# Gate and upper halves of an FFN as seven products of block sums, in two phases with the activations in DRAM

## The chip, the cores and the metric

The kernel runs on one core of a Trainium2 chip. The metric is the device time of one execution in microseconds (us). It is taken over several runs, and the median stands for the kernel. One further execution is profiled.

## The reference

One layer of a hybrid decoder: a normalised input goes through one projection into a chunk-gating group, a stick-breaking attention and a forgetting attention, their outputs through one output projection, and then through a dense SwiGLU FFN. The change touches the FFN alone, for 1024 prompt rows and 64 sample rows (1088 tokens), a model width of 1024 and an inner width of 2816:

```python
def swiglu(x, w_in, w_out):
    h = x @ w_in
    return (jax.nn.silu(h[..., :D_FF]) * h[..., D_FF:]) @ w_out
...
        yp = yp + swiglu(rms_norm(yp, g_ffn[l]), w_ffn_in[l], w_ffn_out[l])
...
        ys = ys + swiglu(rms_norm(ys, g_ffn[l]), w_ffn_in[l], w_ffn_out[l])
...
    y_prompt = rms_norm(yp, g_final)
```

## The kernel before

Every large product is made of three matmuls, since each fp32 operand is split into a rounded part ("hi", an ACT cast) and the remainder ("lo", a DVE or POOL subtraction): hi by hi, hi by lo and lo by hi. PE accumulates them in a PSUM bank. The order of the instructions on every engine is set by a scheduler that simulates the program; the code gives the order of buffers and the priorities.

Ahead of the FFN the output projection ends (`product`, tile prod, L1147 to L1150): the residual sits in y, nine row tiles of 128 tokens in SBUF. `step` normalises a finished row tile (L190, L196) and `spread` transposes it on PE (L204), casts it on ACT into xh2 (L206) and subtracts on DVE into xl2 (L207). The last weights of the output projection are loaded as wor (L1134), cast on ACT (L1137) and split on DVE (L1138).

The FFN loop runs over the 22 slices of 128 inner columns, in 11 pairs (FCH = 2). For each slice, the gate's and the upper weights (128x1024, tile fraw_) are loaded by SP's queue (L1308), cast by ACT (fh, L1311), and the remainder taken by DVE (fl, L1312). For each of three token chunks (384, 384 and 320 columns) and both halves there are 8 times 3 matmuls into a bank of tag fgu (L1326 to L1328). ACT takes the silu of the gate's bank (L1331), DVE multiplies the upper bank by it (L1332), ACT casts the product into g_h (L1333) and POOL takes the remainder g_l (L1335). After two slices the output weights, split in the same way, follow: for nine row tiles and two halves of 512 columns the matmuls fout (L1359, L1360 and L1362), 104 for each pair, and DVE adds each bank to y (L1363). Tag fgu has three of the eight banks, fout and the transposes the other five. Behind the last pair the squares, the scale and the output rows follow (L1279 to L1296), DVE and POOL sharing the rows.

Of the kernel before, what the change touches and what calls it, by code (L numbers as in the profile page):

```python
# [10 lines left out]
F32 = mybir.dt.float32  # L11
# [7 lines left out]
D = 1024  # L19
# [11 lines left out]
FCH = 2  # L31
_TC = {"schedule_with_timeline_sim": True}
# [64 lines left out]
def tile_decode_step(ctx, tc, x_prompt, x_sample, cache_sb_k, cache_sb_v, cache_fox_k, cache_fox_v,  # L97
# [55 lines left out]
    fsn = dr.tile([6, 64], F32, name="fsn")  # L153

# [924 lines left out]
    def merge(mp, y):  # L1079
# [63 lines left out]
        def product(gi, i, hf, xs, ws, o, meanwhile=None):  # L1143
# [9 lines left out]
            V.scalar_tensor_tensor(y[0:n, i, hs], pm[0:n], rr[0:n, gi, i:i + 1], y[0:n, i, hs], op0=OP.mult,  # L1153
# [21 lines left out]
        for j, gi in enumerate(ORDER):  # L1175
            for hf in range(2):
                nxt = ORDER[j + 1] if hf and j < 2 else None
                for ci in range(3):
# [40 lines left out]
    ypool = pool(ctx, "ypool", side="right")  # L1219
    y = ypool.tile([128, NTILE, D], F32, name="y")  # L1220
# [3 lines left out]
    G.memset(y[64:128, 8], 0.0)  # L1224
# [21 lines left out]

    def step(lag):
        if whole_:
            i = whole_.pop(0)
            if i == 8:  # L1250
                t = xin.tile([128, D], F32, name="xs2", tag="xs2", bufs=XSB)
                A.copy(t[0:64], y[64:128, 8])
                V.tensor_tensor(y[0:64, 8], y[0:64, 8], t[0:64], op=OP.add)
                G.memset(y[64:128, 8], 0.0)
            xn.append((i, norm(y[:, i], rows(i), gfb, xin)))
        if len(xn) > lag:
            i, x2 = xn.pop(0)
            spread(x2, rows(i), i, xh2, xl2)
# [4 lines left out]
    whole(8)  # L1263
    pmp.close()
    wfst = ExitStack()
    wf = pool(wfst, "wf", side="right")

    sums = {}

    def square(i, hf):  # L1270

        n, hs = rows(i), slice(hf * 512, hf * 512 + 512)
        jk = wf.tile([128, D], F32, name="fraw_", bufs=3)
        if i == 8:
# [23 lines left out]
    for f0 in range(0, NFF, FCH):  # L1298
# [4 lines left out]
        for ff in range(f0, f0 + nf):  # L1303
            ws_ = []
            for half in range(2):
                c0 = half * DFF + ff * 128
                raw = wf.tile([128, KT, 128], F32, name="fraw_", bufs=3)
                S.dma_start(raw, w_ffn_in[0, :, c0:c0 + 128].rearrange("(k p) c -> p k c", p=128))  # L1308
                h_ = wf.tile([128, KT, 128], F32R, name="fh", bufs=3)
                l_ = wf.tile([128, KT, 128], F32R, name="fl", bufs=3)  # L1310
                A.copy(h_, raw)  # L1311
                V.tensor_tensor(l_, raw, f(h_), op=OP.subtract)  # L1312
                ws_.append((h_, l_))
# [83 lines left out]
```

## Time and profile before

| | us |
|---|---|
| three runs | 1647.5, 1649.11, 1650.43 (median 1649.11) |
| profiled execution, its own time | 1652.82 |
| its span, first to last instruction | 1651.1 |
| PE busy in the span | 1559.6 |
| DVE, ACT, POOL busy | 862.3, 627.7, 474.7 |
| mean granted clock of TensorE, as a share | 0.976 |

Busy time is the sum of an engine's instructions. Matmuls overlap in the records: one is shown from its start to a modelled end, though the next starts earlier, so their pace is read from starts. The timeline gives start, length, engine, line, and what was written and read, with the buffer's number left out. A bracket at a row's end tells how long the engine was idle and what released it.

### The profile page before, as it was taken

What the parts mean: (1) busy time and instruction counts of PE and PEld (TensorE: products, weight loads), DVE (VectorE), ACT (ScalarE), POOL (GpSimd) and SP (SyncE); (2) the same over time, 40 slices, a digit from 0 to 9 for tenths busy, and PEclk for the clock granted to TensorE, in tenths of its full rate; (3) what the DMA queues carried; (4) which work ended last, traced back from release to release, by engine and by line L of the source; (5) the groups of instructions that cost most, each with busy time, mean ns of one, the idle gap of its engine ahead of it and who ended that gap; (6) DMA issues with size and microseconds to landing.
All of it is one profiled execution on the core that took longest, in us unless ns stands there. A gap on an engine that the chain in (4) does not pass through costs nothing.

```text
span 1651.1 us, 23878 instructions
## 1 busy us (share of the span) xinstructions
PE 1559.6 (94%) x8980; PEld 1439.6 (87%) x8980; DVE 862.3 (52%) x1565; ACT 627.7 (38%) x1291; POOL 474.7 (29%) x596
## 2 busy tenths in 40 slices
PE   6999999798799989888999999999999999999997
PEld 6999998697588878777889999898998989999895
DVE  5433369767688978787683332413333242333316
ACT  6424256555477878744362112120111212111114
POOL 1203275546355654464211001010100101010013
PEclk9999999999899989999999999999999999999999
DMA  5255565447867865854222111111110111111002
GB/s 174 56 168 180 187 187 147 114 134 236 222 204 227 234 182 165 290 175 127 88 83 84 39 38 52 44 45 41 52 52 26 52 51 42 36 52 51 26 1 108
DMA packets 137303, 184.54 MB, mean 112 GB/s; under 512 B 17844, under 2 KB 110372, under 8 KB 137188
## 3 DMA queue, kind: packets, MB, share of 16 engines
q1 hardware_dynamic: 127924, 132.48, 27.1%
q0 software_dynamic: 9264, 50.53, 9.6%
q8 instruction: 71, 1.16, 0.3%
q14 instruction: 44, 0.36, 0.1%
HBM read 147.50 MB, written 35.47 MB: 111 GB/s over the span
## 4 chain that ended last, share of the span: by engine, by line
PE 52%; DVE 2%; DMA 2%; issue 1%; POOL 0%; ACT 0%; SPq 0%; DVEq 0%; POOLq 0%; ACTq 0%
PE fgu L1326 11%; PE fgu L1328 11%; PE fgu L1327 11%; PE fout L1360 5%; PE fout L1359 5%; PE fout L1362 5%; PE prod L1147 1%; PE prod L1148 1%; DMA lr<-linv 1%; PE prod L1150 1%; DMA wor<-in_w_o_dram 0%; DVE fl L1294 0%; PE spread L204 0%; DVE vh L812 0%; DVE cr L1107 0%
## 5 line engine op out<-in xcount | busy, mean ns | idle before, releaser
L1328 PE MATMUL fgu<-xh,fl 128*128 128x384 f32 (+1 forms) x1056 | 345.9, 328 | 1.0 <-DVE fl L1312 1.0
L1326 PE MATMUL fgu<-xh,fh 128*128 128x384 f32 (+1 forms) x1056 | 345.4, 328 | 0.8 <-ACT xh L206 0.5
L1327 PE MATMUL fgu<-xl,fh 128*128 128x384 f32 (+1 forms) x1056 | 345.7, 327 | 0.0
L1335 POOL TENSOR_TENSOR g_l<-sl,g_h 128x384 fp32r<-128x384 f32 (+1 forms) x66 | 75.1, 1138 | 672.9 <-ACT g_h L1333 672.9
L1363 DVE TENSOR_TENSOR y<-fout,y 128x512 f32<-128x512 f32 x198 | 135.6, 690 | 127.9 <-PE fout L1362 115.9
L1326 PEld LDWEIGHTS fgu<-xh,fh 128*128 128x128 f32 x1056 | 198.1, 188 | 2.9 <-ACT xh L206 0.8
L1328 PEld LDWEIGHTS fgu<-xh,fl 128*128 128x128 f32 x1056 | 198.3, 188 | 2.2 <-DVE fl L1312 1.3
L1327 PEld LDWEIGHTS fgu<-xl,fh 128*128 128x128 f32 x1056 | 198.3, 188 | 0.7
L1332 DVE TENSOR_TENSOR sl<-fgu,sl 128x384 f32<-128x384 f32 (+1 forms) x66 | 35.3, 535 | 301.4 <-PE fgu L1328 301.4
L1360 PE MATMUL fout<-fol,g_h 128*128 128x512 f32 x396 | 156.6, 395 | 0.0
L1359 PE MATMUL fout<-foh,g_h 128*128 128x512 f32 x396 | 156.5, 395 | 0.0
L1362 PE MATMUL fout<-foh,g_l 128*128 128x512 f32 x352 | 139.1, 395 | 0.0
L812 POOL TENSOR_TENSOR vh<-vr,vh 128x384 fp32r<-128x384 f32 x96 | 102.4, 1083 | 80.0 <-ACT vh L811 59.7
L1333 ACT CAST g_h<-sl 128x384 fp32r<-128x384 f32 (+1 forms) x66 | 32.6, 493 | 184.6 <-DVE sl L1332 184.6
L743 PE MATMUL sqk<-kt,qz 128*128 128x512 f32 x288 | 99.3, 439 | 3.0 <-DVE ats L800 1.2
L286 PE MATMUL pqk<-xh,wh 128*128 128x384 f32 (+1 forms) x288 | 97.0, 337 | 1.2 <-DVE pvt L599 0.6
L287 PE MATMUL pqk<-xl,wh 128*128 128x384 f32 (+1 forms) x288 | 95.5, 333 | 0.0
L288 PE MATMUL pqk<-xh,wl 128*128 128x384 f32 (+1 forms) x288 | 94.8, 333 | 0.0
L1360 PEld LDWEIGHTS fout<-fol,g_h 128*128 128x128 f32 x396 | 74.3, 188 | 16.7
L1359 PEld LDWEIGHTS fout<-foh,g_h 128*128 128x128 f32 x396 | 74.3, 188 | 16.7
L582 PE MATMUL apv<-at,vv 128*128 128x256 f32 x432 | 76.2, 299 | 10.3 <-DVE hl L302 4.8
L572 DVE TENSOR_TENSOR at<-atr,at 128x512 fp32r<-128x512 f32 (+2 forms) x144 | 76.3, 543 | 16.1 <-ACT at L571 15.5
(436 smaller groups left out, 3302.3 us busy)
## 6 DMA issues: line engine op xcount, KB each, us to landing
qq<-qs SPq DMA_DIRECT2D x36, 256.0 KB
wraw<-in_w_in_dram SPq DMA_DIRECT2D x20, 384.0 KB
kk<-ks SPq DMA_DIRECT2D x24, 256.0 KB
vs<-vt SPq DMA_DIRECT2D x16, 384.0 KB
vv<-vs SPq DMA_DIRECT2D x12, 512.0 KB
wor<-in_w_o_dram SPq DMA_DIRECT2D x22, 256.0 KB
qs<-hl SPq DMA_DIRECT2D x12, 384.0 KB
ks<-hl SPq DMA_DIRECT2D x12, 384.0 KB
```

The costliest lines, as they stand in the source:

```text
L286: T.matmul(pm[:, 0:n], lhsT=wh, rhs=xh[:, k, o], start=k == 0, stop=False)
L287: T.matmul(pm[:, 0:n], lhsT=wh, rhs=xl[:, k, o], start=False, stop=False)
L288: T.matmul(pm[:, 0:n], lhsT=wl, rhs=xh[:, k, o], start=False, stop=k == KT - 1)
L743: T.matmul(pz, lhsT=queries(p, a, si), rhs=kts[t][p][:, b], start=si == 0 and p == 0 and n_ == 0, stop=si == 1 and p == 2 and n_ == 2)
L812: (V if t >= 16 and j in VL else G).tensor_tensor(vh[:, 1], vrs[t][:, j], f(vh[:, 0]), op=OP.subtract)
L1326: T.matmul(pm[:, 0:n], lhsT=h_[:, k], rhs=xh2[:, k, o], start=k == 0, stop=False)
L1327: T.matmul(pm[:, 0:n], lhsT=h_[:, k], rhs=xl2[:, k, o], start=False, stop=False)
L1328: T.matmul(pm[:, 0:n], lhsT=l_[:, k], rhs=xh2[:, k, o], start=False, stop=k == KT - 1)
L1359: T.matmul(pm, lhsT=gh[q][:, o], rhs=wh2[q][:, hs], start=q == 0, stop=False)
L1360: T.matmul(pm, lhsT=gh[q][:, o], rhs=wl2[q][:, hs], start=False, stop=i == 8 and end)
L1362: T.matmul(pm, lhsT=gl[q][:, o], rhs=wh2[q][:, hs], start=False, stop=end)
L1363: V.tensor_tensor(y[:, i, hs], pm, y[:, i, hs], op=OP.add)
```

## The change

The two halves of the FFN's input weights are cut into blocks: the 8 groups of 128 model rows into two blocks of four, gate and upper columns as the two column blocks, and the 1088 tokens into two halves of 544 columns (HT). A block product of two by two by two blocks needs eight products; here it is made of seven products of sums of blocks, with additions on both sides. The code names them q = 1 to 7.

Weight sums: `wsum` makes four sums of 128x512 on POOL for each slice j. `split` makes hi and lo of the seven weight operands (ACT cast L1321 and DVE subtraction L1322, 128x512 each). Token sums: `token_sums` makes, once, the operands of q = 5, 6, 7 and 4 in tiles th and tl, from the spread tokens, which now lie in four tiles each of xh and xl; 4 block rows by 2 column chunks, DVE and POOL taking parts (L1420 to L1434). Products: `product` (L1335 to L1337) makes 12 matmuls of 272 columns in an fgu bank, for seven q and two chunks c, so 14 products for each slice and 308 in all. `first` holds q = 1, 2, 3, `second` q = 6, 5, 7, 4; in the loop `first` of slice j + 1 stands ahead of `second` of slice j. The results are joined: L1353 (ga), L1364 (u2), L1367 (t), L1376 (u3), L1378 and L1385 on DVE, all reading a bank; two additions, one of them beside each silu of ACT, and two multiplications in each chunk on POOL. The bank of q = 5 is read twice, by L1367 and, once q = 7 is there, by L1378.

Two phases: the finished activations ga and gb of a slice are stored to DRAM (gs, two transfers per slice), and y's row tiles 0 to 7 are stored to ysc as soon as they are normalised, and their SBUF room is released for the weights. After the 22 slices all of phase one's room is released; y comes back (tiles z0 to z7, L1480), and the second phase loads for each slice the output weights (L1519) and its activations (L1521), splits them (L1524 to L1530), and runs the fout matmuls and additions as before, in pairs.

```diff
 FCH = 2
+HT = NTOK // 2
+RAWB, WSB, FOB = 2, 8, 4
...
+    gs = [dr.tile([128, NTOK], F32, name=f"gs{j}") for j in range(NFF)]
+    ysc = [dr.tile([128, D], F32, name=f"ysc{i}") for i in range(8)]
...
+            if i < 8:
+                S.dma_start(ysc[i], y[i])
...
+    def wsum(j):
+        ga_, up = raws[j]
+        g1, g2, u1, u2 = ga_[:, 0:4], ga_[:, 4:8], up[:, 0:4], up[:, 4:8]
...
+        G.tensor_tensor(s1, u1, u2, op=OP.add)
+        G.tensor_tensor(s2, s1, g1, op=OP.subtract)
+        G.tensor_tensor(s4, g2, s2, op=OP.subtract)
+        G.tensor_tensor(s3, g1, u1, op=OP.subtract)
+        sums[j] = {1: g1, 2: g2, 3: s4, 4: u2, 5: s1, 6: s2, 7: s3}
+
+    def split(j, q):
...
+        A.copy(x[:, 0], src)
+        V.tensor_tensor(x[:, 1], src, f(x[:, 0]), op=OP.subtract)
...
+    NP = ((0, HT // 2), (HT // 2, HT))
+    FIRST, SECOND = (1, 2, 3), (6, 5, 7, 4)
...
+    def product(j, q, c):
...
+        pm = bank([128, 512], "fgu")
+        for k in range(4):
+            T.matmul(pm[:, 0:b - a], lhsT=w[:, 0, k], rhs=hi[:, k, a:b], start=k == 0, stop=False)
+            T.matmul(pm[:, 0:b - a], lhsT=w[:, 0, k], rhs=lo[:, k, a:b], start=False, stop=False)
+            T.matmul(pm[:, 0:b - a], lhsT=w[:, 1, k], rhs=hi[:, k, a:b], start=False, stop=k == 3)
...
+    def second(j, q, c):
+        pm = product(j, q, c)
...
+        elif q == 5:
+            t = temp("t", 3)
+            V.tensor_tensor(t, pm, held[j, c, "u2"], op=OP.add)
...
+            G.tensor_tensor(o, t, held.pop((j, c, 3)), op=OP.add)
+            A.activation(o, o, AF.Silu)
+            held[j, c, 5] = pm
+        elif q == 7:
+            u = held[j, c, "u3"] = temp("u3", 2)
+            V.tensor_tensor(u, pm, held.pop((j, c, "u2")), op=OP.add)
+            t = temp("t", 3)
+            V.tensor_tensor(t, held.pop((j, c, 5)), u, op=OP.add)
+            o = gts[j, 1][:, a:b]
+            G.tensor_tensor(o, o, t, op=OP.mult)
+            if c == 1:
+                S.dma_start(gs[j][:, HT:], gts.pop((j, 1)))
...
+    def token_sums(c):
...
+        for k in range(4):
...
+            V.tensor_tensor(b12, *two(x12, k), op=OP.add)
...
+            V.tensor_tensor(t1, b12, h, op=OP.subtract)
+            V.tensor_tensor(t1, t1, l, op=OP.subtract)
+            less(t2, x22, t1, k, V)
+            part(t1, k, 5, V)
+            part(t2, k, 6, V)
...
+            less(t3, x22, b12, k, G)
+            part(t3, k, 7, G)
...
+            less(t4, x21, t2, k, V)
+            part(t4, k, 4, G)
...
+    for j in range(NFF):
+        if j + 1 < NFF:
+            for q in FIRST:
+                for c in range(2):
+                    first(j + 1, q, c)
+            for q in SECOND:
+                split(j + 1, q)
+        if j + 2 < NFF:
+            wsum(j + 2)
+        for q in SECOND:
+            for c in range(2):
+                second(j, q, c)
...
+    for i in range(8):
+        S.dma_start(y[i], ysc[i])
...
+            raw = fo.tile([128, D], F32, name="wor2", bufs=3)
+            S.dma_start(raw, w_ffn_out[0, ff * 128:ff * 128 + 128, :])
+            graw = fo.tile([128, NTOK], F32, name="gr", bufs=3)
+            S.dma_start(graw, gs[ff])
...
+            A.copy(g_h[:, 0:NTOK], graw)
...
+            (V if ff % 2 else G).tensor_tensor(g_l, graw[:, 0:SP_], f(g_h[:, 0:SP_]), op=OP.subtract)
```

The order of the instructions, for three places. First the steady loop. On DVE, before, one pair's gate and upper part (sl is the gated product, fl and fol the remainders of weights):

```order
L1312 TENSOR_TENSOR fl<-fraw__10227,fh 128x1024 [waits DMAHW6_49,PE_49,Activation_49]
L1332 TENSOR_TENSOR sl<-fgu,sl 128x320 [waits PE_49,Activation_49]
L1312 TENSOR_TENSOR fl<-fraw__10547,fh 128x1024 [waits DMAHW1_49,Activation_49]
L1332 TENSOR_TENSOR sl<-fgu,sl 128x384 [waits PE_49,Activation_49]
L1332 TENSOR_TENSOR sl<-fgu,sl 128x384 [waits DVE_49,PE_49,Activation_49]
L1312 TENSOR_TENSOR fl<-fraw__10553,fh 128x1024 [waits DMAHW2_49,PE_49,Activation_49]
L1332 TENSOR_TENSOR sl<-fgu,sl 128x320 [waits PE_49,Activation_49]
L1312 TENSOR_TENSOR fl<-fraw__10733,fh 128x1024 [waits DMAHW4_49,Activation_49]
L1363 TENSOR_TENSOR y<-fout,y 128x512 [waits PE_49] x18
```

On DVE now, the second half of one slice, with u for u2 and u3:

```order
L1322 TENSOR_TENSOR ws<-raw_10680,ws 128x512 [waits DMAHW0_49,Activation_49]
L1367 TENSOR_TENSOR t<-fgu,u_10808 128x272 [waits DVE_49,PE_49]
L1367 TENSOR_TENSOR t<-fgu,u_10823 128x272 [waits DVE_49,PE_49]
L1322 TENSOR_TENSOR ws<-raw_10680,ws 128x512 [waits Activation_49]
L1376 TENSOR_TENSOR u_10873<-fgu,u_10808 128x272 [waits PE_49]
L1378 TENSOR_TENSOR t<-fgu,u_10873 128x272 [waits DVE_49]
L1376 TENSOR_TENSOR u_10891<-fgu,u_10823 128x272 [waits PE_49]
L1378 TENSOR_TENSOR t<-fgu,u_10891 128x272 [waits DVE_49,Pool_49]
L1322 TENSOR_TENSOR ws<-s_10790,ws 128x512 [waits Activation_49]
L1385 TENSOR_TENSOR t<-fgu,u_10873 128x272 [waits PE_49,Pool_49]
L1385 TENSOR_TENSOR t<-fgu,u_10891 128x272 [waits PE_49,Pool_49]
L1322 TENSOR_TENSOR ws<-s_10788,ws 128x512 [waits Activation_49]
```

Eight short instructions that read banks stand among the splits of 128x512, and the first L1376, which reads the first bank of q = 7, stands behind a split that waits for ACT.

On PE, before, the border between two of the products (fgu_11154 and fgu_11184 are banks' tiles):

```order
L1326 MATMUL fgu_11154<-xh2_9284,fh_11068 128x384
L1327 MATMUL fgu_11154<-xl2_9285,fh_11068 128x384
L1328 MATMUL fgu_11154<-xh2_9284,fl_11069 128x384
L1326 MATMUL fgu_11184<-xh2_9284,fh_11062 128x320 [waits DVE_49]
L1327 MATMUL fgu_11184<-xl2_9285,fh_11062 128x320
L1328 MATMUL fgu_11184<-xh2_9284,fl_11063 128x320
```

On PE now, the border between the two chunks of q = 7, which lie in the same bank, since the two banks of q = 5 are still held:

```order
L1335 MATMUL fgu_11378<-xh01_9331,ws_11040 128x272
L1336 MATMUL fgu_11378<-xl01_9332,ws_11040 128x272
L1337 MATMUL fgu_11378<-xh01_9331,ws_11040 128x272
L1335 MATMUL fgu_11396<-xh01_9331,ws_11040 128x272 [waits DVE_49]
L1336 MATMUL fgu_11396<-xl01_9332,ws_11040 128x272
L1337 MATMUL fgu_11396<-xh01_9331,ws_11040 128x272
```

The first matmul of the second chunk waits for DVE (L1376 of the first chunk), where before the bank had been handed back earlier.

Second, the entry of the FFN. On DVE, before, among the last row tiles (xs the normalised row, xl the spread remainder):

```order
L1153 SCALAR_TENSOR_TENSOR y<-prod,fraw,y 128x512 [waits PE_49]
L196 SCALAR_TENSOR_TENSOR xs_9824<-y,rs,gfb 128x1024 [waits Pool_49]
L1332 TENSOR_TENSOR sl<-fgu,sl 128x384 [waits PE_49]
L207 TENSOR_TENSOR xl_9285<-spread,xh_9284 128x4x128 [waits Activation_49]
L137 TENSOR_SCALAR ss<-ss 128x1 [waits Activation_49]
L207 TENSOR_TENSOR xl_9285<-spread,xh_9284 128x4x128 [waits PE_49,Activation_49]
L196 SCALAR_TENSOR_TENSOR xs_9997<-y,rs,gfb 128x1024 [waits Pool_49]
L207 TENSOR_TENSOR xl_9285<-spread,xh_9284 128x4x128 [waits Activation_49]
L1253 TENSOR_TENSOR y<-y,xs_10018 64x1024 [waits DVE_49,Activation_49]
```

On DVE now, the stretch where the first products of `second` wait (u and t the sums, th and tl their parts):

```order
L1364 TENSOR_TENSOR u_10549<-fgu,p_10104 128x272 [waits PE_49,Pool_49]
L1425 TENSOR_TENSOR t<-xh_9327,u_10379 128x272 [waits DVE_49]
L1434 TENSOR_TENSOR u_10400<-u_10400,xl_9326 128x272 [waits DVE_49]
L1420 TENSOR_TENSOR tl_10196<-u_10379,th_10195 128x272 [waits Activation_49]
L1426 TENSOR_TENSOR t<-t,xl_9328 128x272 [waits DVE_49]
L1425 TENSOR_TENSOR u_10401<-xh_9329,u_10400 128x272 [waits DVE_49]
L1420 TENSOR_TENSOR tl_10198<-u_10400,th_10197 128x272 [waits Activation_49]
L1426 TENSOR_TENSOR u_10401<-u_10401,xl_9330 128x272 [waits DVE_49]
L1425 TENSOR_TENSOR t<-xh_9327,u_10401 128x272 [waits DVE_49,Pool_49]
L1420 TENSOR_TENSOR tl_10196<-u_10401,th_10195 128x272 [waits Activation_49]
L1426 TENSOR_TENSOR t<-t,xl_9328 128x272 [waits DVE_49]
L1367 TENSOR_TENSOR t<-fgu,u_10549 128x272 [waits PE_49,Pool_49]
```

The token sums, their remainders and waits on POOL stand between the two additions L1364 and L1367 of the first slice.

Third, SP's queue. Before, the loop's weights follow one another:

```order
L1308 DMA fraw__10547<-in_w_ffn_in_dram 128x8x128 [waits DMAHW2_49,DVE_49]
L1308 DMA fraw__10553<-in_w_ffn_in_dram 128x8x128 [waits DMAHW7_49,DVE_49]
L1345 DMA fraw__10727<-in_w_ffn_out_dram 128x1024 [waits DMAHW6_49,DMAHW3_49,DVE_49]
L1308 DMA fraw__10733<-in_w_ffn_in_dram 128x8x128 [waits DMAHW4_49,DMAHW1_49,DVE_49]
L1308 DMA fraw__10739<-in_w_ffn_in_dram 128x8x128 [waits DMAHW2_49,DVE_49]
L1345 DMA fraw__10913<-in_w_ffn_out_dram 128x1024 [waits DMAHW4_49,DVE_49]
```

Now, between the phases (gs_118 is the last slice's store, gs_97 the first slice's):

```order
L1382 DMA gs_118<-gb 128x544 [waits DMAHW0_49,Pool_49]
L1519 DMA wor_16000<-in_w_ffn_out_dram 128x1024 [waits DMAHW1_49,PE_49]
L1521 DMA gr<-gs_97 128x1088 [waits DMASW5_49,DMAHW2_49,DMASW0_49,PE_49]
L1519 DMA wor_16013<-in_w_ffn_out_dram 128x1024 [waits DMAHW3_49]
L1389 DMA gs_118<-ga 128x544 [waits DMAHW4_49,Pool_49]
L1521 DMA gr<-gs_98 128x1088 [waits DMAHW5_49,DMASW0_49]
L1519 DMA wor_16166<-in_w_ffn_out_dram 128x1024 [waits DMAHW6_49]
L1521 DMA gr<-gs_99 128x1088 [waits DMAHW7_49]
L1514 DMA gfin<-in_g_final_dram 128x1024 [waits DMAHW0_49]
L1519 DMA wor_16179<-in_w_ffn_out_dram 128x1024 [waits DMAHW1_49,DVE_49]
L1480 DMA z_15983<-ysc_119 128x1024 [waits DMAHW2_49,PE_49]
```

The second phase's first loads stand behind the store of gb, and further loads behind the store of ga of the last slice.

## Rows read from the trace of the kernel before

**Rows 1.** The page's first part: busy us, share, instructions.

```profile
PE 1559.6 (94%) x8980; PEld 1439.6 (87%) x8980; DVE 862.3 (52%) x1565; ACT 627.7 (38%) x1291; POOL 474.7 (29%) x596
```

**Rows 2.** The chain that ended last, its shares by line.

```profile
PE fgu L1326 11%; PE fgu L1328 11%; PE fgu L1327 11%; PE fout L1360 5%; PE fout L1359 5%; PE fout L1362 5%; PE prod L1147 1%; PE prod L1148 1%; DMA lr<-linv 1%; PE prod L1150 1%; DMA wor<-in_w_o_dram 0%; DVE fl L1294 0%; PE spread L204 0%; DVE vh L812 0%; DVE cr L1107 0%
```

**Rows 3.** Windows view, columns as PE, PEld, DVE, ACT, POOL, PEclk, DMA, GB/s.

```profile
1500.00:1600.00 100.00, 100.00 (x565) 95.24 (x564) 26.59 (x36) 15.85 (x27) 10.48 (x12) 1.00 0.11 32
```

**Rows 4.** Timeline of PE, fout (start us, us, engine, line).

```profile
897.88 0.40 PE L1359 MATMUL fout<-foh,g_h 128*128 128x512 f32 x1
...
1614.41 0.39 PE L1359 MATMUL fout<-foh,g_h 128*128 128x512 f32 x1
...
1638.45 0.40 PE L1362 MATMUL fout<-foh,g_l 128*128 128x512 f32 x1
```

**Rows 5.** Timeline of PE: 256 columns in ptok, 384 in fgu.

```profile
46.24 0.28 PE L332 MATMUL ptok<-wh,xh 128*128 128x256 f32 x1
...
49.70 0.29 PE L334 MATMUL ptok<-wh,xl 128*128 128x256 f32 x1
...
879.40 0.33 PE L1326 MATMUL fgu<-xh,fh 128*128 128x384 f32 x1
...
880.44 0.33 PE L1326 MATMUL fgu<-xh,fh 128*128 128x384 f32 x1
```

**Rows 6.** Groups by line with shapes apart (busy us, mean ns).

```profile
L1332 DVE TENSOR_TENSOR sl<-fgu,sl 128x320 f32<-128x320 f32 x22 | 10.8, 492 | 36.4 <-PE fgu L1328 36.4
...
L572 DVE TENSOR_TENSOR at<-atr,at 128x256 fp32r<-128x256 f32 x24 | 9.8, 409 | 0.4 <-ACT at L571 0.3
...
L1138 DVE TENSOR_TENSOR wol<-wor,woh 128x512 fp32r<-128x512 f32 x22 | 15.8, 729 | 4.8 <-ACT woh L1137 4.5
...
L1137 ACT CAST woh<-wor 128x512 fp32r<-128x512 f32 x22 | 13.2, 620 | 24.8 <-PE prod L1150 10.9 <-DMA wor<-in_w_o_dram 6.8 <-PE prod L1147 5.2
...
L1331 ACT ACTIVATE sl<-fgu 128x320 f32<-128x320 f32 x22 | 9.4, 427 | 2.4 <-PE fgu L1328 2.4
...
L558 POOL TENSOR_TENSOR at_g<-at_g,at_s 128x1024 f32<-128x1024 f32 x6 | 12.0, 2008 | 2.7 <-DVE at_s L556 2.3
...
L558 POOL TENSOR_TENSOR at_g<-at_g,at_s 128x512 f32<-128x512 f32 x6 | 6.6, 1092 | 3.1 <-DVE at_s L556 2.8
```

**Rows 7.** Timeline near the end, DVE and POOL.

```profile
1636.31 1.27 DVE L1294 SCALAR_TENSOR_TENSOR fl<-y,rs,gfin 128x1024 f32<-128x1024 f32 x1
...
1637.95 2.36 POOL L1292 TENSOR_TENSOR fh<-fh,gfin 128x1024 f32<-128x1024 f32 x1
...
1638.10 3.29 DVE L1294 SCALAR_TENSOR_TENSOR fl<-y,rs,gfin 128x1024 f32<-128x1024 f32 x1
```

**Rows 8.** Timeline of PE where the FFN begins.

```profile
842.83 0.45 PE L1326 MATMUL fgu<-xh,fh 128*128 128x384 f32 x1 [0.39 <-ACT fh L1311]
...
853.54 0.40 PE L1148 MATMUL prod<-wol,ch 128*128 128x512 f32 x1
...
867.05 0.74 PE L1326 MATMUL fgu<-xh,fh 128*128 128x320 f32 x3 [0.21 <-ACT xh L206]
```

**Rows 9.** Timelines of ACT and SP's queue at the same place.

```profile
844.38 0.38 SPq L1308 DMA_DIRECT2D fraw__10221<-in_w_ffn_in_dram  x1
...
845.61 1.16 ACT L1137 CAST woh<-wor 128x512 fp32r<-128x512 f32 x2
848.16 1.05 ACT L1311 CAST fh<-fraw__10221 128x1024 fp32r<-128x1024 f32 x1 [1.39 <-DMA fraw__10221<-in_w_ffn_in_dram]
```

**Rows 10.** Windows view again, one early and one behind a pause of PE.

```profile
6.00:8.00 2.00, 0.91 (x5) 0.92 (x6) 0.75 (x1) 0.49 (x2) 0.24 (x1) 1.00 1.03 384
690.00:695.00 5.00, 5.00 (x18) 4.25 (x18) 3.24 (x7) 3.60 (x8) 3.51 (x4) 0.57 1.03 407
```

More of the change, by code (lines that the diff above doesn't have):

```diff
@@ L1223, in tile_decode_step @@
     ends = []
-    G.memset(y[64:128, 8], 0.0)
+    G.memset(y8[64:128], 0.0)
     whole_ = []
@@ L1262, in tile_decode_step, with wload @@
     ends[0](xin)
-    whole(8)
     pmp.close()
+    while xn:
+        step(0)
+    pyy.close()
     wfst = ExitStack()
     wf = pool(wfst, "wf", side="right")
+    raws, parts, sums, held, gts = {}, {}, {}, {}, {}
+    def wload(j):
+        raws[j] = []
+        for half in range(2):
+            c0 = half * DFF + j * 128
+            r = wf.tile([128, KT, 128], F32, name=f"raw{half}", bufs=RAWB)
+            S.dma_start(r, w_ffn_in[0, :, c0:c0 + 128].rearrange("(k p) c -> p k c", p=128))
+            raws[j].append(r)
@@ new lines, in temp, with first @@
+    def temp(name, bufs):
+        return wf.tile([128, HT // 2], F32, name=name, bufs=bufs)
+    def first(j, q, c):
+        pm = product(j, q, c)
+        a, b = NP[c]
+        if q == 1:
+            if c == 0:
+                gts[j, 0] = wf.tile([128, HT], F32, name="ga", bufs=2)
+            p = held[j, c, 1] = temp("p1", 4)
+            A.copy(p, pm)
+        elif q == 2:
+            o = gts[j, 0][:, a:b]
+            V.tensor_tensor(o, pm, held[j, c, 1], op=OP.add)
+            A.activation(o, o, AF.Silu)
+        else:
+            p = held[j, c, 3] = temp("p3", 4)
+            A.copy(p, pm)
@@ new lines, in tile_decode_step @@
+    XB[1], XB[2], XB[3] = ((XH[x], XL[x]) for x in ((0, 0), (1, 0), (1, 1)))
+    wload(0)
+    wload(1)
+    wsum(0)
+    for q in FIRST:
+        split(0, q)
+    for q in (1, 2):
+        for c in range(2):
+            first(0, q, c)
+    first(0, 3, 0)
+    whole(8)
+    while whole_ or xn:
+        step(0)
+    pxin.close()
+    ft = pool(pfp, "ft", side="left")
+    for q in (6, 5, 4):
+        XB[q] = (ft.tile([128, 4, HT], F32R, name=f"th{q}"), ft.tile([128, 4, HT], F32R, name=f"tl{q}"))
@@ new lines, in tile_decode_step @@
+    for q in SECOND:
+        split(0, q)
+    token_sums(0)
+    wsum(1)
+    for q in FIRST:
+        split(1, q)
+    first(0, 3, 1)
+    token_sums(1)
+    wload(2)
+    for j in range(NFF):
+        if j + 1 < NFF:
+            for q in FIRST:
+                for c in range(2):
[4 more added lines that the diff above has]
+            wsum(j + 2)
+        for q in SECOND:
+            for c in range(2):
+                second(j, q, c)
+        del raws[j]
+        if j + 2 < NFF:
+            for q in FIRST:
+                split(j + 2, q)
+        if j + 3 < NFF:
+            wload(j + 3)
@@ L1268, in tile_decode_step @@
+    wfst.close()
+    pfp.close()
+    fo = pool(ctx, "fo", side="left")
+    ypool = pool(ctx, "ypool2", side="right")
+    y = [ypool.tile([128, D], F32, name=f"z{i}") for i in range(8)] + [y8]
+    for i in range(8):
+        S.dma_start(y[i], ysc[i])
+    gfin = fo.tile([128, D], F32, name="gfin")
     sums = {}
@@ L1303, in tile_decode_step @@
         for ff in range(f0, f0 + nf):
[L1304 to L1313, printed above, removed]
```

141 lines of the change are left out of this document (86 added, 55 removed).

## The prediction, made before the changed kernel ran

> **What bounds the kernel now.** The page's busy times come first: PE is at work for 94% of the span [rows 1]. The chain of waits says that this is the path: its largest shares are the three lines of the gate and upper products, 11% each, and then the three of the output product, 5% each [rows 2]. The windows confirm it where the change is made: in the loop PE is busy for all of 100 us at a granted clock of 1.00 (its upper level, 2.4 GHz), while DVE has 27, ACT 16 and POOL 10 [rows 3]. So a matmul less is time less, as long as nothing else comes to wait. The pair's period is read from the first fout of the first and the last pair, (1614.41 - 897.88) / 10 = 71.65 us; the 104 fout of the last pair run from 1614.41 to the last start at 1638.45 and one pace more, some 24.27 us [rows 4]. This leaves 47.39 us for a pair's gate and upper products, or 521.3 us for eleven. Counted back from the first fout, a full loop began in effect at 897.88 - 47.39 = 850.5, although products had been mixed with the last row tiles from 842.83 on and ran densely from 867.05 [rows 4, 8].
>
> **What the removal gives.** 22 x 2 x 24 x 3 = 3168 matmuls of 384 and 320 columns become 308 x 12 = 3696 of 272. Their pace: 29 steps from 46.24 to 49.70 make 0.119 us for 256 columns, six from 879.40 to 880.44 make 0.173 for 384 [rows 5]. 272 lies at 0.126 between them, so a product of 12 takes 1.51 us and all of them 465.4: 55.9 us less than 521.3. This is what the change can win; smaller matmuls cost next to nothing, by these rows.
>
> **The loop.** PE's order shows one border without slack: the two chunks of q = 7 share a bank, as q = 5 holds the other two. The second chunk may start only when DVE's L1376 has emptied the bank. The last matmul outlasts its pace (0.28 us shown for 256 columns [rows 5]); then the addition from a bank at 272 columns, between 0.409 and 0.492 us [rows 6], say 0.44; with two handovers the distance is 0.79 where 0.126 would do: 0.66 us lost. That needs DVE to be there. It stands behind a split, which waits for ACT's cast, which waits for the silu of q = 5, which waits for POOL's addition. From the end of the first q = 5: 0.44 + POOL 0.68 (between 512 and 1024 columns POOL adds 0.00179 us for a column, which gives 0.66 for 272) + silu 0.43 + cast 0.62 + split 0.73 [rows 6] and handovers come to 3.1 us, and L1376 is due 3.0 us after it. There is no room: any delay of DVE or POOL is PE's. I take 0.9 us for each slice (0.66 to 1.4), or 18.9 for the 21 slices behind the first. The other borders have one or two products, 1.5 to 3.0 us, for an evacuation of 0.5, and I cost them at nothing; if DVE were late by more than that, this cover would go.
> The Trainium skill says in "Perfetto Trace Analysis", section "Optimizing Tensor Performance", that independent groups of matmuls should rotate through different PSUM banks so that emptying one overlaps the next. By that rule this border is a stall, and it agrees with the sum above; no row of before shows such a border.
>
> **The entry.** This is the large term. The weights of the FFN can no longer be loaded early: they take the room of the residual and of the output projection, so their load stands behind the last product, whose own weights wor were there by 845.61, when ACT casts them [rows 9]. Now the stores of y stand ahead of wor on SP's queue; 847 for 845.6. From that cast to the last output product took 8 us (853.54 [rows 8]); the weights then need 3.8 us (issued 844.38, cast at 848.16 [rows 9]), with a second load behind, and the first product starts near 847 + 15 = 862. From 847 + 13 on DVE has, by its order, until the addition L1364 of the second q = 6 chunk: 15 splits at 0.73 = 10.9 us, 72 token-sum additions and remainders at 0.44 = 31.7, a last row tile's 1.3 and 12 instructions from banks 5.3, 49 us. PE has but 16 products, 24 us, to run there, since `second` of the first slice needs the sums of both chunks. It finishes the 20 products of `first` (two slices) and `second` (one) about 7 us behind that addition: 847 + 13 + 49 + 7 = 916 without any other delay.
> POOL works beside it: 12 weight sums at 1.09 and 32 token sums at 0.68, 35 us. Near the end of before a DVE instruction on two SBUF operands that takes 1.27 alone took 3.29 while POOL's 2.36 ran from 0.15 us earlier: it waited for all the rest of it [rows 7]. If each of POOL's instructions holds up DVE so, the part of the 35 us that falls into DVE's stretch and is not beside the bank reads, some 27, is added: 943. Part falls into DVE's own waits for ACT and POOL, so I take two thirds, 18: the 20 products are done at 934 (916 to 950). Undisturbed they would have ended at 850.5 + 20 x 1.51 = 880.7, so the entry costs 53 us and eats the gain by itself. Idle PE also lowers its clock: one window behind pauses shows 0.57 [rows 10], near the lower level of 1.2 GHz; for a few products that is 3 to 5 us, within the range.
> In "SBUF — State Buffer", section "Who interferes with whom", the Trainium skill says that a DVE instruction with two SBUF inputs and a GpSimd instruction that reads SBUF exclude one another. By this rule the entry ends at 943, not 934; rows 7 agree with it.
>
> **The transition.** Phase two's first loads stand on SP behind the store of gb, further ones behind that of ga of the last slice, and reading comes behind the release of all room. A load took 3.8 us [rows 9], then a cast of about 1.1 (1.16 for two halves [rows 9]) and subtractions beside it: the first fout comes some 6 us behind the last product. The tiles z, 4.2 MB, with weights and activations 8.7 MB, need 23 us at the 384 GB/s of an early window [rows 10] and are wanted one each 2.7 us, so they mostly keep up. I take 6 us, 4 to 14. In the loop the added traffic, two loads of 512 KB and 557 KB of stores each 21 us, is 75 GB/s, far below 384, and costs nothing.
>
> **The sum**, against the profiled span of 1651.1: entry until 934; 288 products x 1.511 = 435.2; loop 18.9; transition 6; eleven times 24.27 = 267.0; tail behind the last fout 1651.1 - 1638.7 = 12.4 [rows 4]. Together 1673.5. The median of the runs stood 2.0 below this span, so 1671.5: slower by 22 us, or 1.4%.
>
> **The rivals.** (A) DVE and POOL do not exclude each other in short instructions. For it: the rows that show it plainly are of 1024 columns, and the 128x512 splits of rows 6 have a mean of only 0.73; against it: rows 7. Then the entry ends at 916 and the loop loses 0.66: 1651.1 - 18 - 5 from the sum above give 1650 and, less 2, 1648: no change. (B) Faster: the token sums are cheaper than the instructions by which I priced them. Those read a bank; the sums read SBUF alone, and no row has 272 columns. At 0.30 us in place of 0.44 the 72 take 10 us less, and without exclusion the entry ends at 906: 1638. It decides from about 0.40 downward, and only together with no exclusion; the rows of SBUF subtractions, 729 ns for 512 columns [rows 6], speak against it. (C) Much slower: exclusion holds in the loop too. Each slice has 4 x 1.09 + 6 x 0.68 = 8.4 us of POOL and 12 x 0.44 + 7 x 0.73 = 10.4 of DVE in 21 us, and the chain ahead of L1376 has no slack, so the stall could be 2 us: 23 us more, with the entry at 943: 1704. For it: rows 7; against it: 12 of DVE's 19 read a bank.
>
> **How the numbers follow.** The sum and its near neighbours: 0.62. A: 0.14, half of it within 0.2% (3.3 us, what a measurement of this kernel can tell), the rest split between the sides. B: 0.11. C: 0.13. The range leaves out the far part of B and of C: low 1643, high 1698. Faster by over 0.2%: 0.14 (B and some of A); same: 0.10; slower: 0.76.
>
> **What would show it.** Right: gaps of PE before `second` of the first slice, summing to about 50 us between 854 and 934, with token-sum rows of DVE as releasers and lengths above 0.6 us while POOL runs; one gap of 0.7 to 1 us in each slice, ahead of the second q = 7 chunk, released by L1376; a distance of 21.2 + 0.9 us from slice to slice; a gap of about 6 us between the phases; fout pairs 24.27 apart. Wrong: a period of 21.2 us would mean that the border of q = 7 is hidden; a second slice begun near 900 would sink the entry's term; matmuls further apart than 0.126 would shrink the 55.9, and gaps behind loads in phase two would make the transition a longer one.

## The result, and the profile after

The changed kernel takes 1664.27 us (median of 1662.85 to 1666.89) against 1648.55 us for the kernel before beside it: a ratio of 1.0096, with a 95% interval from 1.0078 to 1.0113. It is slower by 16 us, where 22 had been forecast, and inside the range. Its profiled execution took 1662.85 us, with a span of 1661.1.

The page's first part of the kernel after, which answers to [rows 1]:

```profile
PE 1516.3 (91%) x9508; PEld 1392.7 (84%) x9508; DVE 1096.3 (66%) x1958; ACT 716.1 (43%) x1501; POOL 691.2 (42%) x793
```

PE has 43 us less to do and still finishes later: its share of the span fell from 94% to 91%. What it waits for stands in the page's costliest groups, whose last part is the idle time ahead of a group and what ended it:

```profile
L1335 PE MATMUL fgu<-xh,ws 128*128 128x272 f32 x704 | 209.2, 297 | 21.0 <-DVE u L1376 16.5
...
L1335 PE MATMUL fgu<-th,ws 128*128 128x272 f32 x528 | 155.3, 295 | 12.4 <-ACT th L1419 12.2
...
L1542 PE MATMUL fout<-foh,g_h 128*128 128x512 f32 x396 | 155.1, 392 | 6.8 <-POOL g_h L1529 6.8
```

The first row is the border of q = 7 in the loop (L1376), the second the token sums at the entry (L1419 is the cast in `part`), the third the transition between the phases. In the windows view the entry and the loop, again as PE, PEld, DVE, ACT, POOL, PEclk, DMA, GB/s:

```profile
860.00:930.00 70.00, 44.03 (x218) 37.96 (x219) 62.68 (x99) 25.70 (x62) 42.53 (x41) 0.66 0.14 42
1000.00:1200.00 200.00, 192.95 (x1521) 190.98 (x1520) 105.33 (x172) 65.18 (x136) 91.08 (x92) 1.00 0.23 73
```

At the entry PE was busy for 44 of 70 us at a mean granted clock of 0.66, so much of it at the lower level (1.2 GHz), while DVE was busy for 63. Before, the same 70 us had PE at 69.8 and a clock of 1.00:

```profile
860.00:930.00 70.00, 69.79 (x389) 64.61 (x388) 30.05 (x40) 15.65 (x25) 7.79 (x9) 1.00 0.22 64
```

What PE waited for in the changed kernel stands in the brackets of two rows from inside the first product that needs token sums. The two rows behind them lie ten steps apart, so a matmul of 272 columns took 0.227 us there, against 0.1255 in the loop:

```profile
889.68 0.59 PE L1336 MATMUL fgu<-tl,ws 128*128 128x272 f32 x1 [4.07 <-DVE tl L1420]
...
894.49 0.60 PE L1335 MATMUL fgu<-th,ws 128*128 128x272 f32 x1 [3.98 <-ACT th L1419]
...
918.29 0.43 PE L1336 MATMUL fgu<-xl,ws 128*128 128x272 f32 x1
...
920.56 0.43 PE L1337 MATMUL fgu<-xh,ws 128*128 128x272 f32 x1
```

The loop's border on PE's timeline, in two consecutive slices, and what DVE, POOL and ACT did ahead of the first:

```profile
945.32 0.39 PE L1335 MATMUL fgu<-xh,ws 128*128 128x272 f32 x1 [0.78 <-DVE u L1376]
967.46 0.40 PE L1335 MATMUL fgu<-xh,ws 128*128 128x272 f32 x1 [0.79 <-DVE u L1376]
```

```profile
943.87 1.05 DVE L1322 TENSOR_TENSOR ws<-raw,ws 128x512 fp32r<-128x512 f32 x1 [0.35 <-ACT ws L1321]
944.84 0.42 DVE L1376 TENSOR_TENSOR u<-fgu,u 128x272 f32<-128x272 f32 x1
```

```profile
943.60 0.77 POOL L1371 TENSOR_TENSOR gb<-t,p 128x272 f32<-128x272 f32 x1 [0.74 <-DVE t L1367]
```

The period is 967.46 - 945.32 = 22.14 us. The split ahead of L1376 waited for ACT and then took 1.05 us, where one without POOL beside it takes 0.68; POOL's addition was running when it began. L1376 started behind it at 944.84, and PE was released.

Stretch by stretch, from the last matmul of the three-part products of the output projection (L1150 before, L1154 after), by PE's timeline; the first row is of the kernel before, the others are of the kernel after:

```profile
837.91 0.40 PE L1150 MATMUL prod<-woh,cl 128*128 128x512 f32 x1
```

```profile
828.76 0.40 PE L1154 MATMUL prod<-woh,cl 128*128 128x512 f32 x1
...
1382.85 0.29 PE L1337 MATMUL fgu<-th,ws 128*128 128x272 f32 x1
...
1389.95 0.80 PE L1542 MATMUL fout<-foh,g_h 128*128 128x512 f32 x1 [6.81 <-POOL g_h L1529]
...
1650.82 0.39 PE L1545 MATMUL fout<-foh,g_l 128*128 128x512 f32 x1
```

| stretch | forecast | measured |
|---|---|---|
| that matmul to the end of the first 20 products | 934 - 837.9 = 96.1 | 98.9 |
| 288 products with the border of q = 7 | 435.2 + 18.9 = 454.1 | 455.3 |
| transition | 6 | 7.0 |
| second phase | 267.0 | 261.1 |
| tail | 12.4 | 10.0 |
| together | 835.6 | 832.3 |

(The end of the first 20 products is taken from the steady loop: the second q = 7 chunk of slice 1 starts at 945.32, less one period of 22.14, and three products of 1.51 behind it, which gives 927.7; the 21st product itself starts at 927.81. The last product of the phase ends at 1383.0.) The same stretch was 813.2 us before, so the change costs 19 us here. The matmul from which it is counted lay at 837.9 in the trace of before and at 828.8 in that of after; of these 9 us the run with y in nine tiles, below, tells.

### The profile page after: what moved, and what is told of

It is laid out like the page before. It is cut to its first block, busy times and chain, and to the rows that moved or that the text cites. A ratio compares the mean times of both kernels' runs of the same rounds, so it can differ in the third digit from the quotient of the medians.

```text
span 1661.1 us, 26462 instructions
## 1 busy us (share of the span) xinstructions
PE 1516.3 (91%) x9508; PEld 1392.7 (84%) x9508; DVE 1096.3 (66%) x1958; ACT 716.1 (43%) x1501; POOL 691.2 (42%) x793
## 4 chain that ended last, share of the span: by engine, by line
PE 44%; DVE 8%; DMA 2%; ACT 2%; POOL 1%; issue 1%; SPq 0%; DVEq 0%; POOLq 0%; ACTq 0%
PE fgu L1335 8%; PE fgu L1337 8%; PE fgu L1336 8%; PE fout L1542 5%; PE fout L1543 5%; PE fout L1545 5%; DVE ws L1322 2%; PE prod L1151 1%; PE prod L1152 1%; DMA lr<-linv 1%; PE prod L1154 1%; POOL gb L1371 1%; ACT ws L1321 1%; DVE t L1367 1%; DVE tl L1420 1%
## 5 line engine op out<-in xcount | busy, mean ns | idle before, releaser
L1335 PE MATMUL fgu<-xh,ws 128*128 128x272 f32 x704 | 209.2, 297 | 21.0 <-DVE u L1376 16.5
L1337 PE MATMUL fgu<-xh,ws 128*128 128x272 f32 x704 | 206.0, 293 | 2.2 <-DVE ws L1322 2.2
L1336 PE MATMUL fgu<-xl,ws 128*128 128x272 f32 x704 | 205.6, 292 | 0.1
L1335 PE MATMUL fgu<-th,ws 128*128 128x272 f32 x528 | 155.3, 295 | 12.4 <-ACT th L1419 12.2
L1546 DVE TENSOR_TENSOR z<-fout,z 128x512 f32<-128x512 f32 x176 | 117.7, 687 | 66.9 <-PE fout L1545 66.2
L1336 PE MATMUL fgu<-tl,ws 128*128 128x272 f32 x528 | 154.8, 293 | 6.5 <-DVE tl L1420 6.5
L1335 PEld LDWEIGHTS fgu<-xh,ws 128*128 128x128 f32 x704 | 135.4, 192 | 27.3 <-DVE u L1376 21.4
L1337 PE MATMUL fgu<-th,ws 128*128 128x272 f32 x528 | 154.6, 293 | 0.0
L1337 PEld LDWEIGHTS fgu<-xh,ws 128*128 128x128 f32 x704 | 135.2, 192 | 2.9 <-DVE ws L1322 2.9
L1336 PEld LDWEIGHTS fgu<-xl,ws 128*128 128x128 f32 x704 | 136.0, 193 | 0.4 <-DVE xl L1269 0.4
L1322 DVE TENSOR_TENSOR ws<-s,ws 128x512 fp32r<-128x512 f32 x88 | 81.8, 933 | 50.3 <-ACT ws L1321 47.6
L1335 PEld LDWEIGHTS fgu<-th,ws 128*128 128x128 f32 x528 | 101.2, 192 | 14.5 <-ACT th L1419 14.0
L1336 PEld LDWEIGHTS fgu<-tl,ws 128*128 128x128 f32 x528 | 101.5, 192 | 8.2 <-DVE tl L1420 8.2
L1337 PEld LDWEIGHTS fgu<-th,ws 128*128 128x128 f32 x528 | 101.5, 192 | 0.0
L1321 ACT CAST ws<-s 128x512 fp32r<-128x512 f32 x88 | 54.1, 621 | 106.2 <-PE fgu L1337 106.2
```

The source lines that it names most:

```text
L1321: A.copy(x[:, 0], src)
L1322: V.tensor_tensor(x[:, 1], src, f(x[:, 0]), op=OP.subtract)
L1335: T.matmul(pm[:, 0:b - a], lhsT=w[:, 0, k], rhs=hi[:, k, a:b], start=k == 0, stop=False)
L1336: T.matmul(pm[:, 0:b - a], lhsT=w[:, 0, k], rhs=lo[:, k, a:b], start=False, stop=False)
L1337: T.matmul(pm[:, 0:b - a], lhsT=w[:, 1, k], rhs=hi[:, k, a:b], start=False, stop=k == 3)
L1546: V.tensor_tensor(y[i][:, hs], pm, y[i][:, hs], op=OP.add)
```

## The experiments

**The border of q = 7.** Two ways to give its second chunk a free bank. One changes the order:

```diff
-        for q in SECOND:
-            for c in range(2):
-                second(j, q, c)
+        for q, c in ((6, 0), (6, 1), (5, 0), (7, 0), (5, 1), (7, 1), (4, 0), (4, 1)):
+            second(j, q, c)
```

> In the loop the second chunk of q = 5 now stands between the two chunks of q = 7 (order 6, 6, 5, 7, 5, 7, 4, 4), so each bank has one product of 1.51 us to be emptied. Theory (the border of q = 7 waits because its two chunks share one bank): the period of a slice falls from 22.14 to about 21.17 us, the 0.79 us gap ahead of the second q = 7 chunk is gone, and the time falls by some 21 us, from 1664 to 1643. Rival (DVE is late there because of POOL, ACT and the split in its queue, wherever the bank is): a gap of the same size moves to the next product and the time stays within 5 us of 1664.

The other keeps the order and moves q = 5 into idle banks:

```diff
-        pm = bank([128, 512], "fgu")
+        pm = bank([128, 512], "fout" if q == 5 else "fgu")
```

> The two products of q = 5 go into two of the five banks that lie idle in phase one; the order of the products stays. Theory (shared bank): as with the other order, period 21.17 us and 1643 us, although L1376 still stands behind the split in DVE's queue. Rival (DVE late in its queue): the gap stays at 0.5 us or more in each slice, and the time above 1653.

Measured: 1638.69 us with the other order, 0.9963 of before (0.9947 to 0.9979), and 1633.76 us with the other banks, 0.9920 (0.9894 to 0.9945), where the changed kernel stood at 1.0096. The windows view of the loop, first of the one with the order, then of the one with the banks:

```profile
1000.00:1200.00 200.00, 200.00 (x1595) 200.00 (x1594) 110.77 (x181) 68.60 (x143) 95.25 (x96) 1.00 0.25 79
```

```profile
1000.00:1200.00 200.00, 200.00 (x1595) 200.00 (x1595) 109.07 (x182) 68.73 (x143) 94.31 (x95) 1.00 0.25 79
```

PE is busy for all of 200 us where it had been for 193, and nowhere in the loop does a row show it idle. In the second kernel DVE still meets L1376 behind the split:

```profile
1000.43 1.19 DVE L1322 TENSOR_TENSOR ws<-raw,ws 128x512 fp32r<-128x512 f32 x1 [0.21 <-ACT ws L1321]
1001.55 0.43 DVE L1376 TENSOR_TENSOR u<-fgu,u 128x272 f32<-128x272 f32 x1
```

So the shared bank made the wait, and DVE's lateness only its size. By the ratios the order gave 22 us, where 21 had been expected, and the banks 29. In their profiles phase one, counted from the same matmul, is 26 and 31 us shorter. The loop gives 21 of these (288 products took 433.9 us with the other order, 455.3 with the changed kernel); the rest lies in the entry, which is shorter in both. With the banks PE was idle there for 20 of the 70 us in place of 26, which nothing here explains in full:

```profile
860.00:930.00 70.00, 50.15 (x284) 44.45 (x283) 67.41 (x104) 27.64 (x66) 46.45 (x45) 0.78 0.14 42
```

The Trainium skill's sentence in "Perfetto Trace Analysis", section "Optimizing Tensor Performance", that independent groups should rotate through different banks, agrees with both runs.

**What holds the entry.** First, POOL's part of the token sums is given to DVE (`less` for t3, `part` for t3 and t4):

```diff
-            less(t3, x22, b12, k, G)
-            part(t3, k, 7, G)
+            less(t3, x22, b12, k, V)
+            part(t3, k, 7, V)
...
-            part(t4, k, 4, G)
+            part(t4, k, 4, V)
```

> POOL's 32 token-sum instructions are given to DVE, which then has 104 in place of 72; nothing else is changed. Theory (DVE with two SBUF operands and POOL shut one another out, so POOL's help costs DVE its whole length): DVE's token sums fall back to 0.43 us shown, 0.35 apart, except beside the weight sums; 32 more cost 11 us and some 25 of waiting go, so the entry ends 10 to 16 us sooner and the time is 1648 to 1655. Rival (DVE is bound by the number of its instructions): the entry ends 11 us later, 1675.

Measured: 1660.39 us, 1.0091 of before (1.0057 to 1.0125), by its time no different from the changed kernel: neither the time of the theory nor that of the rival came. Its profile shows the entry 5.6 us shorter (from the same matmul to the second q = 7 chunk, 87.1 us in place of 92.8): the sign of the theory, at half its size or less. How DVE's instructions look beside POOL and without it, in the changed kernel:

```profile
876.27 0.43 DVE L1425 TENSOR_TENSOR u<-xh,u 128x272 f32<-128x272 f32 x1
876.62 0.43 DVE L1420 TENSOR_TENSOR tl<-u,th 128x272 fp32r<-128x272 f32 x1
...
893.90 1.00 DVE L1433 TENSOR_TENSOR u<-u,xh 128x272 f32<-128x272 f32 x1
894.83 0.99 DVE L1425 TENSOR_TENSOR t<-xh,u 128x272 f32<-128x272 f32 x1
```

```profile
893.64 0.97 POOL L1420 TENSOR_TENSOR xl<-t,xh 128x272 fp32r<-128x272 f32 x1
894.57 0.96 POOL L1425 TENSOR_TENSOR t<-xh,u 128x272 f32<-128x272 f32 x1
```

Alone they are 0.43 long and 0.35 apart; while POOL works on SBUF they are 1.00 long, and DVE and POOL go in step. One POOL instruction costs DVE 0.57 us, not the 0.95 that it is shown with. 32 of them are 18 us, and 32 more for DVE at 0.35 are 11, which leaves some 7. The rows bear out that the two engines shut one another out; my 25 us of waiting did not hold, and a gain of 5 us cannot be shown by the runs, whose interval is 11 us wide. In "SBUF — State Buffer", section "Who interferes with whom", the Trainium skill says that a DVE instruction with two SBUF inputs contends with a GpSimd instruction that reads SBUF; the rows agree with it.

Then most of the token sums are left out:

```diff
         for k in range(4):
-            T.matmul(pm[:, 0:b - a], lhsT=w[:, 0, k], rhs=hi[:, k, a:b], start=k == 0, stop=False)
...
+            m = k if q in FIRST else 0
+            T.matmul(pm[:, 0:b - a], lhsT=w[:, 0, k], rhs=hi[:, m, a:b], start=k == 0, stop=False)
...
-        for k in range(4):
+        for k in range(1):
             b12, t1, t2 = temp("u2", 2), temp("u3", 2), temp("u3", 2)
```

> The changed kernel with only the first of the four block rows of the token sums made; the products q = 6, 5 and 4 use it for all four, and q = 7 the first row of its operand, so the output is not the reference's; matmuls and everything behind the entry stay. Theory (the entry is the token sums): 54 DVE instructions at 0.35 us and 24 of POOL, each holding DVE for 0.56, go, some 32 us; PE's gaps of 27 us and its low clock there nearly vanish: 1630 to 1638. Rival (splits and ACT): 1650 or more.

Measured: 1625.65 us, 0.9894 of before (0.9869 to 0.9918), 33 us below the changed kernel by the ratios (1.0096 - 0.9894 = 0.0202). In the profile phase one, counted from the same matmul, ends 33.7 us sooner (520.4 in place of 554.1). So three quarters of the token sums, with ACT's casts of them, cost 33 us of the entry. Undisturbed, its 20 products would have been done 42.8 us behind the matmul from which the table counts (the forecast's 880.7 less 837.9); they took 98.9, so the entry cost 56 us in all. All splits of the weights, and ACT's casts for them, stay in this run, so it was the sums that held PE for most of that time. The other 23 us are not told apart by this run: a quarter of the sums is left, and the first product starts 21.5 us behind the same matmul here too.

**The phases without the seven products.** `wsum`, `split`, `token_sums`, `first` and `second` are replaced by plain products on the same halves and chunks:

```diff
...
+            for k in range(KT):
+                hi, lo = XH[k // 4, th][:, k % 4, a:b], XL[k // 4, th][:, k % 4, a:b]
+                T.matmul(pm, lhsT=w[0][:, k], rhs=hi, start=k == 0, stop=False)
+                T.matmul(pm, lhsT=w[0][:, k], rhs=lo, start=False, stop=False)
+                T.matmul(pm, lhsT=w[1][:, k], rhs=hi, start=False, stop=k == KT - 1)
...
+        A.activation(o, pp[0], AF.Silu)
+        V.tensor_tensor(o, pp[1], o, op=OP.mult)
```

> The same two phases, DRAM for activations and residual, halves and chunks of 272 columns, but with the eight plain products of a block (16 x 24 matmuls for a slice in place of 14 x 12 of q = 1 to 7), without weight sums and token sums. Theory (the seven products save 1/8 of the matmuls, and the entry's token sums and the loop's border take most of it back, while the phases cost some 20 us by themselves): period 24.2 us, entry some 35 us shorter than with the seven, no gap in the loop; 1666 to 1676 us. Rival (the phases cost nothing by themselves, all of the loss is in the seven products): 1655 to 1660.

Measured: 1663.21 us, 1.0108 of before (1.0091 to 1.0125). The time lies between the theory's and the rival's. (A slice has 16 x 12 matmuls here; the 16 x 24 of the expectation is a slip, the period that it gives is right.) With all of the matmuls back the kernel takes the same time as the changed one: as it stands, the seven products win nothing over eight in the same frame. The frame itself costs about 1%. Its matmuls of 272 columns account for half of that: 22 slices of 16 x 12 at 0.1255 us are 530 us, where before the gate and upper products took 521.3. The rest is the start of phase one, late and at first at a low clock. It ends 557.2 us behind the matmul from which the table counts, 27.1 more than its matmuls take, where before this lead was 850.5 - 837.9 = 12.6: 14.5 us more, less 3 that the second phase gains with its transition and 2 at the tail.

**All of it together.** Slices 0 and 1 with plain products, all token sums on DVE beside them, q = 5 in its own banks:

```diff
-    wsum(0)
-    for q in FIRST:
-        split(0, q)
...
+    split8(0)
+    for c in range(2):
+        plain(0, 0, c)
...
+    split8(1)
+    for th, j in ((1, 0), (1, 1)):
+        for c in range(2):
+            plain(j, th, c)
+    wload(2)
+    token_sums(0)
+    for c in range(2):
+        plain(1, 0, c)
...
-    for j in range(NFF):
+    for j in range(2, NFF):
```

> Slices 0 and 1 are made with the eight plain products, which need no token sums, and slices 2 to 21 with the seven; DVE makes all token sums beside the plain products; the two products of q = 5 lie in banks of their own. Theory (the entry is PE waiting for token sums on DVE, nothing else): PE has 48 us of plain products while DVE works, the two slices cost 2 x 3 us more matmuls, so some 25 to 30 us of the entry come back beside the 21 of the loop: phase one ends near 1328 in place of 1383 and the time is 1604 to 1618, faster than the kernel before by about 2%. Rival (the entry is bound by the late weights or by ACT's casts): little more than the banks' gain, 1628 to 1640.

Measured: 1603.95 us, 0.9761 of before (0.9742 to 0.9780), faster than both kernels, with phase one ended at 1326.5. The entry in the windows view of this kernel:

```profile
860.00:930.00 70.00, 70.00 (x560) 69.79 (x560) 59.77 (x134) 29.37 (x70) 17.65 (x13) 1.00 0.23 69
```

DVE is as busy as in the changed kernel (60 us in place of 63), and PE no longer waits: it has products that need no sums, and its clock stays at 1.00. Phase one ends 494.1 us behind the matmul from which the table counts; less 3744 matmuls at 0.1255 and the 12.6 of before, 12 us are left of an entry that had cost 56. That is near the 14.5 of the kernel with plain products alone. It fits the weights that come later, but no run changes their load by itself.

**The 9 us ahead of the FFN.** The kernel before with the residual in nine tiles:

```diff
-    y = ypool.tile([128, NTILE, D], F32, name="y")
+    y = [ypool.tile([128, D], F32, name=f"y{i}") for i in range(NTILE)]
```

> The kernel before with y as nine tiles of 128x1024 in place of one tile, nothing else. The changed kernel's last row-tile products ended 9 us sooner than before's, ahead of all that was costed. Theory A (the separate tiles do it, by another order or fewer waits on y): the output projection ends 5 to 10 us sooner in this profile too, and the time falls by about as much. Theory B (it is the difference of two executions or comes from the FFN's later weight loads): same time within 3 us.

Measured: 1644.75 us, a ratio of 1.0005 (0.9989 to 1.0021), no change. Its own profiled execution had the matmul from which the table counts at 824.0, 14 us sooner than the one of before, without any gain in the time over its runs (1639.26 to 1653.21). The span of this profile, 1637.6, lies 13.5 below that of before, so all of the difference between the two stands ahead of this matmul, and the runs, whose medians agree, do not keep it. In the eight other profiles it lay between 824.1 and 833.4, among them one of the kernel before with 32 bytes of padding (833.4). So a single profile can be off by as much as these 14 us, and by the time Theory B holds. A small part may still be the tiles: all eight kernels with y in separate tiles lie at or below 832.5, the two with y in one tile at 833.4 and 837.9, and the interval leaves room for some 2 us.

**The second phase.** It took 5.9 us less than the same matmuls before. The fout matmuls of the kernel after start closer than those of [rows 4]. Over the 103 steps of the last pair the mean is (1650.82 - 1627.48) / 103 = 0.2266 us, against (1638.45 - 1614.41) / 103 = 0.2334 before:

```profile
1627.48 0.39 PE L1542 MATMUL fout<-foh,g_h 128*128 128x512 f32 x1
...
1650.82 0.39 PE L1545 MATMUL fout<-foh,g_l 128*128 128x512 f32 x1
```

One thing that differs is the address of the stationary operand. By the programs, g_h and g_l lie at odd multiples of 32 bytes before and at multiples of 128 after. In the kernel before:

```diff
+    pad = pool(wfst, "padp", side="right").tile([128, 8], F32, name="pad")
+    G.memset(pad, 0.0)
     wf = pool(wfst, "wf", side="right")
```

> The kernel before with 32 unused bytes ahead of the FFN's tiles in SBUF, which moves fh, fl, g_h and g_l from addresses that are odd multiples of 32 bytes to multiples of 64; nothing else. In the changed kernel's second phase, where g_h and g_l lie at multiples of 64, the fout matmuls start 0.227 us apart, against 0.233 before. Theory (the address of the stationary operand makes this difference): fout at 0.227, 1144 of them 6.5 us less, 0.4% faster. Rival (something else of the second phase does it): fout stays at 0.233 and the time the same within 2 us.

Measured: 1639.61 us, 0.9968 of before (0.9956 to 0.9980), and a mean step of 0.2290 us over the 103 steps of the last pair:

```profile
1605.12 0.40 PE L1361 MATMUL fout<-foh,g_h 128*128 128x512 f32 x1
...
1628.71 0.39 PE L1364 MATMUL fout<-foh,g_l 128*128 128x512 f32 x1
```

The 32 bytes are worth some 5 us to the kernel before, and 0.0044 of the difference of 0.0068 us; what the rest is stays open. With the padding g_h and g_l lie at odd multiples of 64 bytes, not at multiples of 128 as in the kernel after; no run here tries those in the kernel before. The gate and upper products, whose stationary tiles moved by the same 32 bytes, hardly changed: a pair's period fell by 0.48 us, and its 104 fout matmuls account for some 0.45 of that. So it is not a rule for every stationary operand.

## Why the prediction was right, point by point

**What bounds the kernel, and the gain of 55.9.** Right: 272 columns came 0.1255 us apart where 0.126 had been interpolated. A side remark was wrong: I said that smaller matmuls cost next to nothing. The gain had already paid for them; seven eighths of 521.3 would have been 456.1, and the products took 464, so the chunks of 272 cost 8 us.

**The loop.** Right in mechanism and nearly in size: a gap in each slice, released by L1376, and 1.06 us lost for each where 0.9 had been taken (22.14 less 168 x 0.1255). Both cures of the bank removed it. The chain through POOL, ACT and the split made DVE a little later than forecast; rival C, a stall of 2 us, did not come.

**The entry.** The largest term, and right as a sum, 98.9 us for 96.1, by errors that offset: its closeness is luck, its mechanism is not. The addition L1364 of the second chunk, up to which DVE's work was summed, came 88.7 us behind the reference matmul (917.42 - 828.76) for a forecast of 927 - 837.9 = 89.1. DVE's instructions were priced by their length, 0.44, where back to back they start 0.35 apart, 6 us too much for 72. The exclusion was priced too low, as two thirds of 27 us by POOL's lengths. Up to that addition the 72 token sums of DVE are shown with 24 us more than 0.43 each, and the 15 splits with 4 us more than 0.68 each, so some 29 us went where 18 had been taken. POOL's 32 token sums account for some 14 to 18 of them: at 0.57 each they would be 18, an estimate from the rows above, and where DVE took them over 14 of the 29 stay. The weight sums come on top: one DVE instruction of 0.43 us is shown with 5.43 in the changed kernel, from 854.37 on, while POOL went through six instructions without a break:

```profile
854.37 5.43 DVE L1425 TENSOR_TENSOR u<-xh,u 128x272 f32<-128x272 f32 x1
```

```profile
854.10 0.74 POOL L140 TENSOR_TENSOR rs<-ss,nhalf 64x1 f32<-64x1 f32 x1
...
858.75 0.74 POOL L1426 TENSOR_TENSOR t<-t,xl 128x272 f32<-128x272 f32 x1
```

The addition to which the sum ran:

```profile
917.42 0.43 DVE L1364 TENSOR_TENSOR u<-fgu,p 128x272 f32<-128x272 f32 x1
```

The first product started 21.2 us behind the reference matmul, where 24.1 had been allowed. Behind L1364 PE took 10.3 us to the end of the 20 products, not 7, since two more products and a part of the next ran at the lower clock.

One sign came out otherwise than forecast: gaps of PE of about 50 us between 854 and 934. PE was idle for 28 of these 80 us:

```profile
854.00:934.00 80.00, 51.88 (x281) 45.59 (x280) 69.72 (x103) 28.96 (x68) 49.29 (x49) 0.70 0.13 41
```

The rest of what PE lost went into matmuls at the lower clock, 0.227 us each, which filled its waiting; the forecast had named the clock, at 3 to 5 us, but left it out of the sum. The larger gaps also lay inside the first products of `second`, between block rows, and not ahead of them.

Rival A (no exclusion) is refuted by the rows of 5.43 and 1.00 us, which answer to [rows 7]; its sum starts from 1673.5, not from the 1651.1 written there, and its 1650 is right. Rival B asked for cheaper sums and no exclusion; the sums were cheaper, but the other half failed.

**The transition** was 7.0 for 6. **The second phase** was taken over from before as it stood, 267.0; it measured 261.1, a pair 23.57 in place of 24.27, and by the padded kernel the operands' addresses are about two thirds of why. That term I had not thought of as one that could move.

**The median.** Of the 7.2 us between 1671.5 and 1664.3, 3.3 are the sum's own errors. The other 9.1 that the span of after lacks lie ahead of the FFN, in a stretch that the sum had taken from a single execution of before; the medians gave 5.2 of them back, since the forecast took 2.0 off the profiled span and the median of after lies 3.2 above it.

## What to carry to other kernels

A block algorithm that trades matmuls for additions moves work onto the vector engines, and its price is paid where that work comes before any product can run. So the first blocks should be made the plain way, as cover: here that, with banks of their own for results that are held, turned a loss of 1% into a gain of 2.4%. Work split between DVE and POOL, both reading two operands in SBUF, was nearly serial here, and is costed by what one holds up of the other. A difference of two single profiles ahead of the change is checked against the spread of several before it is explained.

## What had not been expected of the hardware

The exclusion of DVE and POOL is not always shared out fairly: POOL kept a DVE instruction waiting for 5 us over six of its own. The address of a stationary operand, an odd multiple of 32 bytes against a multiple of 64, changed the step of matmuls of 512 columns from 0.2334 to 0.2290 us in one product and left another one as it was. The stretch ahead of the FFN, whose code is nearly the same in all of these kernels, moved by 14 us between profiles.
